# Placing the high and low parts of a three-product float32 matmul: weights at multiples of 128 bytes, their partners 64 bytes beyond

## The chip, the cores and the metric

The kernel runs on one core of a Trainium2 chip. The time is that of the device, in microseconds, from the first to the last instruction of one launch, and what is compared is the median of several runs. TensorE multiplies, ScalarE (ACT), VectorE (DVE) and GpSimd (POOL) do elementwise work, SyncE (SP) issues the DMAs. [...]

## The reference, cut to what matters

Two layers run on 1024 prompt tokens and 64 sample tokens of width 1024. Layer 0 mixes tokens with an S5 state space model, layer 1 with RWKV-7. Each is followed by cross-attention to a memory and by an MLP with a squared ReLU, with a residual and a layer norm after each:

```python
out = (z @ p["s5_w_glu_v"][j]) * jax.nn.sigmoid(z @ p["s5_w_glu_g"][j])
...
x = layer_norm(DEEPNORM_ALPHA * x + h, p["ln_g"][i, 0], p["ln_b"][i, 0])
h = memory_cross_attention(x, mem_k[i], mem_v[i], p["xa_w_q"][i], p["xa_w_o"][i])
x = layer_norm(DEEPNORM_ALPHA * x + h, p["ln_g"][i, 1], p["ln_b"][i, 1])
h = sq_relu_mlp(x, p["mlp_w1"][i], p["mlp_w2"][i])      # 1024 -> 4096 -> 1024
```

Everything is float32.

## The kernel before

The activations `x` stay in SBUF, channels on the partitions as 8 panels of 128, the 1088 tokens along the free dimension in four chunks (`CH`): three of 256 tokens and a last one of 320.

A large product isn't done in float32 outright. Each operand is split into a high part rounded to `float32r` and a low part, the rest (`split`, L70, and `wtile`, L74, for weights: ScalarE writes the high part, VectorE or GpSimd the low one). `mm3` (L65) then makes a product of three matmuls, high by high, high by low, low by high, all added up in PSUM:

```python
s.mm(ps, wh, xh, first, False)
s.mm(ps, wh, xl, False, False)
s.mm(ps, wl, xh, False, last)
```

Each of them loads 128 columns of weights (LDWEIGHTS, the row PEld of the profile) and streams 256 or 320 columns of the other operand past them (MATMUL, the row PE). The next weights are loaded while a matmul streams, so at any time TensorE reads two places in SBUF: the moving operand, and the weights of the next matmul. 20,400 of its 28,046 matmuls are such full ones.

The stages, in order: the S5 mixer (to about 318 us); its gated output `glu` (products of X, the split activations `XH`, `XL`, into the banks `pg`); layer 0's attention and MLP (`layer`, `attention`); the RWKV mixer (`rwkv_r`, `rwkv_k`, `rwkv_vg`, `rwkv_solve`, `rwkv_scan`); layer 1's attention and MLP. An MLP runs over 16 iterations of two panels of the hidden width. In each, `up` makes a chunk's hidden activations of X (48 matmuls into `pq`), `split` into `hh` and `hl`, and `down` multiplies those of one chunk before by the second weights (48 matmuls into `pg`) and adds them to the residual. An iteration holds 288 matmuls of 256 columns, half from `up` and half from `down`, and 96 of 320. Attention does the same with `qh`, `ql` (queries), `ph`, `pl` (probabilities) and `oh`, `ol` (heads' outputs); there the queries are the weights, and the memory's keys stream.

The order within an engine is made by the framework's planner, which works from the program's dependencies and its own idea of times; in the MLP it breaks `up` and `down` up into pieces of 3 to 48 matmuls and interleaves them. A tile's place is reused when the last reader of the whole tile is done (`reuse_waits="tile"`). Pools lay their tiles one after the other.

Where the parts lie follows from what was laid before them. In the compiled program of this kernel, the starts of the tiles modulo 128 bytes are:

| stage | moving part | weight part | moving less weight, modulo 128 |
|---|---|---|---|
| glu, layer 0's queries and `up` | XH, XL 96 | wh, wl 32 | 64 |
| layer 0 and 1: `down`, attention's outputs | hh, hl, oh, ol 32 | wh, wl 32 | 0 |
| layer 0 and 1: scores, values | 32 | 32 | 0 |
| rwkv_r, receptance | XH, XL 96 | wh, wl 64 | 32 |
| rwkv_r, decays and gates (64 rows) | hdh, hdl 64 | wah, wal 64 | 0 |
| rwkv_k; rwkv_vg (weights stream) | 96 | 96 | 0 |
| rwkv_scan, output product | oh, ol 96 | wh, wl 96 | 0 |
| layer 1's queries and `up` | XH, XL 32 | wh, wl 32 | 0 |

Slices of a tile (a chunk, a panel, 128 columns of weights) begin at multiples of 128 bytes from its start, so the last column holds for every matmul.

Of the kernel before, what the change touches and what calls it, by code (L numbers as in the profile page):

```python
# [9 lines left out]
F32R = mybir.dt.float32r  # L10
# [5 lines left out]
DRAM = bass.MemoryType.DRAM  # L16

ALPHA = 4.0 ** 0.25
TT = 1088
# [7 lines left out]
class Parts:  # L27
    """tiles side by side in a tile that is not in use yet"""
# [15 lines left out]
class Net:  # L44
# [29 lines left out]
    def wtile(s, src, e=None, cols=1024, rows=128):  # L74
        """A weight panel from DRAM as its two parts."""
        raw = s.raw.tile([128, 1024], F32, name="raw")[:rows, :cols]
        s.load = s.d.dma_start(out=raw, in_=src)
        hi = s.wp.tile([128, 1024], F32R, name="wh", tag="wh")[:rows, :cols]
        lo = s.wp.tile([128, 1024], F32R, name="wl", tag="wl")[:rows, :cols]
        s.a.copy(out=hi, in_=raw)  # L80
        s.lastlo = (e or s.g).tensor_tensor(out=lo, in0=raw, in1=hi.bitcast(F32), op=ALU.subtract)  # L81
        return hi, lo

    def lnexp(s):
        """both ln and exp in ScalarE's tables"""
        s.tc.keep_in_program_order(s.a.preload_act_table_set("natural_log_exp_and_others"))
# [13 lines left out]
    def banks(s, n, W, get):  # L100
        """n panels of width W as (first panel, [128, panels, W]) a bank each"""
        m = 512 // W
        for p in range(0, n, m):
            q = min(m, n - p)
            yield p, q, get(q * W).rearrange("p (j t) -> p j t", j=q)
# [37 lines left out]
    def rnd(s, out, x, scale):  # L143
        """out = the integer nearest to x * scale"""
# [5 lines left out]
    def horner(s, out, r, cs, first):  # L150
        """out = first r^n + cs[0] r^(n-1) + .. without the constant term, times r"""
# [4 lines left out]
    def expx(s, P, out, x):  # L156
        """exp to float32's accuracy"""
# [15 lines left out]
    def sincos(s, P, sn, cs, x):  # L173
        """sin and cos to float32's accuracy"""
# [12 lines left out]
        # i^k: k to -2..2, its cosine 1 - |k|, its sine k (2 - |k|)  # L187
# [14 lines left out]
    def unit(s, P, c, sn):  # L202
        """One Newton step to length 1"""
# [9 lines left out]
    def s5_setup(s, P, sm):  # L213
        """Tables of the powers of a; P holds what stays, sm the temporaries."""
# [18 lines left out]
        # powers 0..8 of a  # L233
# [15 lines left out]
        # f = (a - 1) / lambda  # L249
# [15 lines left out]
        # halves: rows 0..63 the real part, rows 64..127 the imaginary one  # L265
# [9 lines left out]
        # unit rotation by 8 steps, and its powers: lo 0..15, hi 16 * (0..7), two groups of a batch's four in the  # L275
        # rows' first half and two in the second; the sine of all of them with the sign of the first half
# [42 lines left out]
    def s5_tables(s, B, b, Tt, dr):  # L319
        """For four groups, 64 of the 1024 channels: what depends on the weights alone."""  # L320
# [29 lines left out]
        # CA[(half, s), g, tau, c]  # L350
# [11 lines left out]
        # BM[(j, c), g, (half, s)]  # L362
# [10 lines left out]
        # K[(q, c), (tau, c')] and the skip on its diagonal  # L373
# [14 lines left out]
        # rotations e^{i Theta n}, n = 16 hi + lo  # L388
# [23 lines left out]
    def s5_batch(s, B, b, U, CA, BM, T, C2, S2):  # L412
# [3 lines left out]
        # what each chunk brings to the state  # L416
# [29 lines left out]
    def s5_outputs(s, B, dr, U, CA, T, H):  # L446
        """y[(j, c), n], to memory"""
# [13 lines left out]
    def s5_gather(s, B, k, yd, X):  # L461
        """Channels to partitions (of four groups, by channel in the group, then group), the gelu, and its parts."""
# [19 lines left out]
    def s5(s, x, X, filler):  # L482
        """the tables lie in x's place"""
# [29 lines left out]
    def memkv(s, mp, kvd):  # L513
        """a panel at a time, in float32 outright"""
# [45 lines left out]
    def lnsum(s, x, p, c, acc):  # L560
        """adds panels p, p + 1 to the running sum of two columns of panels"""
# [6 lines left out]
    def lndirect(s, x, p, ps):  # L568
        """the last chunk's sum, a panel at a time, one panel late"""
# [16 lines left out]
    def lnsteps(s, x, c, li, acc, X=None, new=None, bank=None, done=None):  # L586
        """Normalise the chunk c of x in place over the channels; its parts into X."""
# [55 lines left out]
    def rsqrt(s, var, bias, eps, W, n=128, tables=True):  # L643
        """(var + eps)^-1/2: a start from the tables, or from the exponent's bits, then Newton steps"""
# [52 lines left out]
    def softmax(s, B, ps, n):  # L697
        """probabilities of the scores ps[128, n, 256]"""
# [14 lines left out]
    def attention(s, l, x, X, kvd, after, B, B1, early, begin):  # L713
        """B, B1: pools that outlive it; early, begin: what may go ahead of the end"""
        tc, v, a, g = s.tc, s.v, s.a, s.g
        s.lnexp()
        with ExitStack() as es:
# [4 lines left out]
            def query(h, c, wq):  # L722
                t0, W = CH[c]
                qh, ql = (Q.tile([128, 2, 256], F32R, name=n) for n in ("qh", "ql"))
# [17 lines left out]
            def probs(ps):  # L742
                pr = s.softmax(B, ps, 2)
                ph, pl = (B1.tile([128, 2, 256], F32R, name=n) for n in ("ph", "pl"))
# [7 lines left out]
            def values(h, c, kh, kl, ph, pl, os):  # L752
                W = CH[c][1]
                oh, ol = (B1.tile([128, 2, 320], F32R, name=n)[:, :, :W] for n in ("oh", "ol"))
# [16 lines left out]
            # the sample's queries, each sequence against its own memory: rows (sequence, 32), two banks' halves  # L771
            def load(nm, h, b):
                """two of the eight"""
# [102 lines left out]
    def layer(s, l, x, X, kvd, norm1, norm2):  # L876
        """attention and MLP, the MLP's first products ahead of the attention's last"""
        tc, v, a, g = s.tc, s.v, s.a, s.g
        NB = 16
        with tc.tile_pool(reuse_waits="tile", name="ab", bufs=2) as B, tc.tile_pool(reuse_waits="tile", name="ab1", bufs=1) as B1, ExitStack() as es:  # L880
# [5 lines left out]
            def up(i, c, w):  # L886
                t0, W = CH[c]
                hh, hl = (M[0].tile([128, 2, 320], F32R, name=n)[:, :, :W] for n in ("hh", "hl"))
# [71 lines left out]
    def shifted(s, P, c, x):  # L960
        """x at t - 1 less x at t, for chunk c, panels 4 h and on"""
# [21 lines left out]
    def mixed(s, i, c, x, d):  # L983
        """chunk c of the i-th token-shift mix, (first k, [128, k's, W]) at a time; d[h]: panels 4 h and on"""
# [7 lines left out]
    def mixes(s, c, x, d, lg, D):  # L992
        """the mixes of the keys and values, and the gates' hidden layer (in float32 outright), to memory"""
# [13 lines left out]
    def remixed(s, i, c, D):  # L1007
        """the same from memory"""
# [5 lines left out]
    def mix(s, m, c, X):  # L1014
        """its parts into X"""
# [4 lines left out]
    def chunked(s, t, q, W):  # L1020
        """[128, q, chunks, 64] of a tile that holds (chunk, q, 64)"""
        return t[:, :q * W].rearrange("p (c e t) -> p e c t", e=q, t=64)
# [4 lines left out]
    def spill(s, D, c, p, q, src, n=64):  # L1027
        """a tile of (chunk, q, n) to the panels from p on of D[chunk, 128, 8, n], and back"""
# [4 lines left out]
    def solve(s, v, M, Th, tm, n, load, store):  # L1033
        """(1 - A)^-1 of 32-blocks, a block in each of n partitions, all transposed"""
# [13 lines left out]
    def rwkv_r(s, x, X, D):  # L1048
        """decays and gates, and the receptance"""
        tc, v, a, g = s.tc, s.v, s.a, s.g  # L1050
        E = math.exp(-0.5)
        with ExitStack() as es:
# [3 lines left out]
            # of the hidden layers: the weights for x, and times the mixes for what the shift adds  # L1056
# [7 lines left out]
            wah, wal = (P.tile([128, 1024], F32R, name=n) for n in ("wah", "wal"))  # L1064
# [3 lines left out]
            hid = [P.tile([128, TT], F32R, name=n) for n in ("hdh", "hdl")]  # L1068

            def lora(c, d):  # L1070
                """the hidden layers, in float32 outright"""
# [59 lines left out]
    def rwkv_k(s, x, X, D):  # L1131
        """keys, the removal's two factors, and how a chunk's removals meet"""
        tc, v, a, g = s.tc, s.v, s.a, s.g
        E = math.exp(-0.5)
        with tc.tile_pool(reuse_waits="tile", name="k1d", bufs=1) as Q, tc.tile_pool(reuse_waits="tile", name="k1u", bufs=2) as T:
# [4 lines left out]
            # a panel's two heads apart  # L1140
# [15 lines left out]
            def unit(p, q, c, ps, cs, al):  # L1156
# [19 lines left out]
                # minus the inverse of the squared length  # L1176
# [5 lines left out]
                # the decays up to the step before  # L1182
# [18 lines left out]
            def removals(p, q, c, pmt, pm, y, kb):  # L1201
                t0, W = CH[c]
                # A_ab of the chunks, [(the chunk's parity, s), head, chunk, t]
# [51 lines left out]
    def rwkv_solve(s, P, D):  # L1255
        """in the place P"""
# [9 lines left out]
        def solve2(p0, e, *place):  # L1266
            """partitions (block, panel, head, chunk)"""
# [13 lines left out]
        def sample():  # L1281
            """partitions (block, panel, head)"""
# [15 lines left out]
    def rwkv_vg(s, x, X, D):  # L1298
        """values and output gates, time on the partitions"""
        tc, v, a, g = s.tc, s.v, s.a, s.g  # L1300
        TL = [(t, min(128, TT - t)) for t in range(0, TT, 128)]
        with tc.tile_pool(reuse_waits="tile", name="v1", bufs=1, side="right") as P:
            hid = [P.tile([128, TT], F32R, name=n) for n in ("hdh", "hdl")]
# [26 lines left out]
    def scan_setup(s, P):  # L1330
        """what the scan holds from its start on"""
        v, g = s.v, s.g
        L, U_, R2 = slice(0, 64), slice(64, 128), slice(32, 64)
        # rows 0..63 a chunk's inverse, rows 64..127 what its removals bring to the outputs
# [3 lines left out]
        # a panel's two heads apart: [(h, j), h, (a, r), panel, t]  # L1338
# [7 lines left out]
        # the bonus' factors, a panel's two heads apart  # L1346
# [6 lines left out]
        # decays over a chunk: of the prompt for rows (64 + j), of the sample for rows (b2, j)  # L1353
# [9 lines left out]
    def rwkv_scan(s, x, D):  # L1363
        """The chunks in order, all the heads at once; head hh = 8 (its half of the panel) + panel."""
        tc, v, a, g = s.tc, s.v, s.a, s.g
        L, U_, R1, R2 = slice(0, 64), slice(64, 128), slice(0, 32), slice(32, 64)
        with tc.tile_pool(reuse_waits="tile", name="r2f", bufs=1) as F, tc.tile_pool(reuse_waits="tile", name="r2", bufs=2) as B, \
# [11 lines left out]
            def heads(hf, get):  # L1379
                """eight heads' places in a bank: (head, its panel, its rows, [128, 64])"""  # L1380
# [4 lines left out]
            def prep(ci, bn=None, own=None):  # L1385
                """own: the sample's tiles"""
# [29 lines left out]
                # what of the chunk meets itself  # L1416
# [9 lines left out]
                # the bonus' weight of each head  # L1426
# [10 lines left out]
                # decayed to the chunk's end, time to partitions  # L1437
# [13 lines left out]
                # the inverse's block off the diagonal  # L1451
# [15 lines left out]
            def chain(ci, E, nxt):  # L1467
                """nxt: where the state goes, and is already without the chunk's own"""
# [21 lines left out]
            def outputs(ci, E, Y):  # L1490
                """into rows of Y: two banks"""
# [13 lines left out]
            def finish(k, Y, bn, y=None):  # L1505
                """group norm, bonus, gate, and channels to partitions"""
# [28 lines left out]
            def store(k, y, n):  # L1535
                """into the parts [k, 128, (a chunk, the sample, a chunk)]"""
# [9 lines left out]
            def out(c, p0):  # L1546
                """two panels of the mixer's output for the chunk c, the sample with the first"""
# [7 lines left out]
                for i in range(2):  # L1555
# [3 lines left out]
                    for h in range(2):  # L1559
                        wh, wl = (W.tile([128, 512], F32R, name=nm, bufs=2) for nm in ("wh", "wl"))  # L1560
# [13 lines left out]
            def norm(c):  # L1574
                """of a finished chunk of the residual"""
# [12 lines left out]
            def sample(S, Q):  # L1588
                """Eight sequences of eight tokens with their own states, a part at a time: places that end with the second
                part, and that stay."""  # L1590
# [342 lines left out]
```

## Time and profile before

| | |
|---|---|
| median of 3 runs | 3892.05 us |
| lowest and highest | 3887.28, 3900.02 us |
| span of the profiled execution | 3890.0 us |
[...]
| PE (matmul) busy | 3556.8 us, 91% |
| PEld (weight load) busy | 3334.9 us, 86% |
| DVE, ACT, POOL busy | 51%, 31%, 36% |

The page has no time of its own for the profiled execution beside its span of 3890.0 us. How to read it: successive matmuls overlap in the trace, because each is shown from its first column to the modelled end of its last. So neither the share of 91% nor the mean of one (280 to 310 ns) is what a matmul costs. In a stream without waits that is the distance from one start to the next, read from the starts of a timeline or from a piece of the chain that has its time and its number of matmuls.

### The profile page before, as it was taken

What the parts mean: (1) busy time and instruction counts of PE and PEld (TensorE: products, weight loads), DVE (VectorE), ACT (ScalarE), POOL (GpSimd) and SP (SyncE); (2) the same over time, 40 slices, a digit from 0 to 9 for tenths busy, and PEclk for the clock granted to TensorE, in tenths of its full rate; (3) what the DMA queues carried; (4) which work ended last, traced back from release to release, by engine and by line L of the source; (5) the groups of instructions that cost most, each with busy time, mean ns of one, the idle gap of its engine ahead of it and who ended that gap; (6) DMA issues with size and microseconds to landing.
All of it is one profiled execution on the core that took longest, in us unless ns stands there. A gap on an engine that the chain in (4) does not pass through costs nothing. (4 is left out here: it accounts for less than half of the span.)

```text
span 3890.0 us, 67671 instructions
## 1 busy us (share of the span) xinstructions
PE 3556.8 (91%) x28046; PEld 3334.9 (86%) x28046; DVE 1980.5 (51%) x3344; ACT 1204.7 (31%) x2299; POOL 1418.1 (36%) x1035
## 2 busy tenths in 40 slices
PE   6669979989999999979987988997899899999997
PEld 4558979979999999968875767997799799999997
DVE  9991174354333333485588656678534633333335
ACT  3662152243112111243572212234422411111113
POOL 5652251143222222433567343344312332222222
PEclk8789999999999999989998877999999999999999
DMA  4444122311111111035576635552222111111111
GB/s 137 127 135 158 33 67 82 112 67 56 44 44 44 44 44 44 30 132 158 171 209 152 192 85 163 144 155 90 88 98 87 66 44 44 44 44 44 44 39 47
DMA packets 270243, 351.22 MB, mean 90 GB/s; under 512 B 109200, under 2 KB 200848, under 8 KB 269168
## 3 DMA queue, kind: packets, MB, share of 16 engines
q1 hardware_dynamic: 269936, 346.89, 29.0%
q8 instruction: 221, 3.62, 0.4%
q14 instruction: 86, 0.70, 0.1%
HBM read 271.80 MB, written 75.01 MB: 89 GB/s over the span
## 5 line engine op out<-in xcount | busy, mean ns | idle before, releaser
L63 PE MATMUL pq<-XH,wh 128*128 128x256 f32 (+1 forms) x2944 | 856.9, 291 | 33.0 <-ACT XH L71 17.0
L57 DVE TENSOR_TENSOR x<-x,pg 128x512 f32<-128x512 f32 (+1 forms) x720 | 435.8, 607 | 840.3 <-PE pg L63 833.8
L63 PE MATMUL pq<-XL,wh 128*128 128x256 f32 (+1 forms) x2944 | 853.4, 290 | 1.6 <-DVE XL L72 1.6
L63 PE MATMUL pq<-XH,wl 128*128 128x256 f32 (+1 forms) x2944 | 851.6, 289 | 1.2 <-POOL wl L81 1.2
L81 POOL TENSOR_TENSOR wl<-raw,wh 128x1024 fp32r<-128x1024 f32 x194 | 467.2, 2418 | 1005.6 <-ACT wh L80 923.9
L63 PEld LDWEIGHTS pq<-XH,wh 128*128 128x128 f32 x2944 | 561.2, 191 | 45.9 <-ACT XH L71 19.8
L63 PE MATMUL pg<-hh,wh 128*128 128x256 f32 (+1 forms) x2048 | 593.8, 290 | 4.9 <-DVE x L57 4.9
L63 PE MATMUL pg<-hl,wh 128*128 128x256 f32 (+1 forms) x2048 | 592.0, 289 | 0.4 <-DVE hl L60 0.4
L63 PE MATMUL pg<-hh,wl 128*128 128x256 f32 (+1 forms) x2048 | 591.5, 289 | 0.0
L63 PEld LDWEIGHTS pq<-XL,wh 128*128 128x128 f32 x2944 | 561.2, 191 | 5.8 <-DVE XL L72 2.5
L63 PEld LDWEIGHTS pq<-XH,wl 128*128 128x128 f32 x2944 | 560.8, 191 | 3.2 <-POOL wl L81 1.8
L80 ACT CAST wh<-raw 128x1024 fp32r<-128x1024 f32 x209 | 215.2, 1047 | 657.3 <-PE pq L63 297.9
L63 PEld LDWEIGHTS pg<-hh,wh 128*128 128x128 f32 x2048 | 385.9, 189 | 6.2 <-DVE x L57 5.3
L63 PEld LDWEIGHTS pg<-hl,wh 128*128 128x128 f32 x2048 | 386.4, 189 | 1.7 <-DVE hl L60 0.8
L63 PEld LDWEIGHTS pg<-hh,wl 128*128 128x128 f32 x2048 | 386.0, 188 | 0.2
L54 POOL TENSOR_TENSOR tm<-tm 128x512 f32<-128x512 f32 (+1 forms) x160 | 146.8, 917 | 532.9 <-ACT tm L893 532.7
L893 ACT ACTIVATE tm<-pq 128x512 f32<-128x512 f32 (+1 forms) x160 | 84.8, 530 | 652.1 <-PE pq L63 632.0
L60 DVE TENSOR_TENSOR hl<-tm,hh 128x512 fp32r<-128x512 f32 (+1 forms) x160 | 101.5, 634 | 197.5 <-POOL tm L54 188.8
L63 PE MATMUL pg<-XH,wh 128*128 128x256 f32 (+1 forms) x640 | 187.2, 293 | 4.8 <-ACT tm L680 2.6
L63 PE MATMUL pg<-XL,wh 128*128 128x256 f32 (+1 forms) x640 | 187.0, 292 | 0.0
L63 PE MATMUL pg<-XH,wl 128*128 128x256 f32 (+1 forms) x640 | 186.5, 291 | 0.5 <-DVE wl L81 0.5
L63 PE MATMUL pg<-ol,wh 128*128 128x256 f32 (+1 forms) x512 | 147.5, 293 | 5.4 <-DVE ol L72 5.4
(474 smaller groups left out, 7049.8 us busy)
## 6 DMA issues: line engine op xcount, KB each, us to landing
raw<-in_w_dram SPq DMA_DIRECT2D x128, 512.0 KB, 3.5
raw<-in_ck_dram SPq DMA_DIRECT2D x32, 512.0 KB, 3.5
raw<-in_cv_dram SPq DMA_DIRECT2D x32, 512.0 KB, 3.5
raw<-in_w_o_dram SPq DMA_DIRECT2D x32, 512.0 KB, 3.6
raw<-in_wk_dram SPq DMA_DIRECT2D x16, 512.0 KB, 4.1
raw<-in_wv_dram SPq DMA_DIRECT2D x16, 512.0 KB, 4.2
raw<-in_wq_dram SPq DMA_DIRECT2D x16, 512.0 KB, 3.5
raw<-in_wo_dram SPq DMA_DIRECT2D x16, 512.0 KB, 5.6
```

The costliest lines, as they stand in the source:

```text
L54: e.tensor_tensor(out=out, in0=a, in1=b, op=ALU.mult)
L57: e.tensor_tensor(out=out, in0=a, in1=b, op=ALU.add)
L60: e.tensor_tensor(out=out, in0=a, in1=b, op=ALU.subtract)
L63: s.lastmm = s.t.matmul(out=out, lhsT=lhsT, rhs=rhs, start=start, stop=stop, **k)
L80: s.a.copy(out=hi, in_=raw)
L81: s.lastlo = (e or s.g).tensor_tensor(out=lo, in0=raw, in1=hi.bitcast(F32), op=ALU.subtract)
L893: a.activation(out=r, in_=ps, func=AF.Relu)
```

## The change

Two helpers place the parts. `even` makes a weight part's tile start at a multiple of 128 bytes. `odd` makes one tile that holds both parts of the other operand, starts it at a multiple of 128 and leaves out the first 16 float32 (64 bytes); the high part comes first, the low part behind it. Every length is a multiple of 128 bytes, so the low part, too, lies 64 bytes beyond a multiple of 128. The queries in the scores, which are the weights of their matmul, are made with `odd`, and the keys and values that they meet with `even`, as panels from `wtile`.

```diff
-        hi = s.wp.tile([128, 1024], F32R, name="wh", tag="wh")[:rows, :cols]
-        lo = s.wp.tile([128, 1024], F32R, name="wl", tag="wl")[:rows, :cols]
+        hi, lo = (s.even(s.wp, 1024, n)[:rows, :cols] for n in ("wh", "wl"))
...
+    def even(s, pool, n, name, **k):
+        return pool.tile([128, n], F32R, name=name, tag=name, align_bytes=128, **k)
+
+    def odd(s, pool, shape, name):
+        n = math.prod(shape[1:])
+        t = pool.tile([128, 2 * n + 16], F32R, name=name, align_bytes=128)[:, 16:]
+        names = "abcd"[:len(shape) - 1]
+        r = f"p ({' '.join(names)}) -> p {' '.join(names)}"
+        return [t[:, i * n:i * n + n].rearrange(r, **dict(zip(names, shape[1:]))) for i in range(2)]
...
-                qh, ql = (Q.tile([128, 2, 256], F32R, name=n) for n in ("qh", "ql"))
+                qh, ql = s.odd(Q, [128, 2, 256], "qhl")
...
-                ph, pl = (B1.tile([128, 2, 256], F32R, name=n) for n in ("ph", "pl"))
+                ph, pl = s.odd(B1, [128, 2, 256], "phl")
...
-                oh, ol = (B1.tile([128, 2, 320], F32R, name=n)[:, :, :W] for n in ("oh", "ol"))
+                oh, ol = (t[:, :, :W] for t in s.odd(B1, [128, 2, 320], "ohl"))
...
-                hh, hl = (M[0].tile([128, 2, 320], F32R, name=n)[:, :, :W] for n in ("hh", "hl"))
+                hh, hl = (t[:, :, :W] for t in s.odd(M[0], [128, 2, 320], "hhl"))
...
-            wah, wal = (P.tile([128, 1024], F32R, name=n) for n in ("wah", "wal"))
+            wah, wal = (s.even(P, 1024, n) for n in ("wah", "wal"))
...
-            hid = [P.tile([128, TT], F32R, name=n) for n in ("hdh", "hdl")]
+            hid = s.odd(P, [128, TT], "hid")
...
-                        wh, wl = (W.tile([128, 512], F32R, name=nm, bufs=2) for nm in ("wh", "wl"))
+                        wh, wl = (s.even(W, 512, nm, bufs=2) for nm in ("wh", "wl"))
...
-                    Xo = [W.tile([128, 8, 576], F32R, name=nm) for nm in ("oh", "ol")]
+                    Xo = s.odd(W, [128, 8, 576], "ohl")
...
-            return [xp.tile([128, 8, TT], F32R, name=nm) for nm in ("XH", "XL")]
+            return n.odd(xp, [128, 8, TT], "X")
```

`hid` is changed in the same way in `rwkv_r` and in `rwkv_vg`. The rest of the diff takes out comments. No instruction is added or taken away in the program's text.

## Rows read from the trace of the kernel before

**Rows 1.** The page's first part: busy us, share of the span, instructions of each engine.

```profile
PE 3556.8 (91%) x28046; PEld 3334.9 (86%) x28046; DVE 1980.5 (51%) x3344; ACT 1204.7 (31%) x2299; POOL 1418.1 (36%) x1035
```

**Rows 2.** Busy time by stretch: length, PE, PEld, DVE, ACT, POOL, PEclk, DMA, GB/s.

```profile
541.00:870.00 329.00, 300.52 (x2323) 276.90 (x2323) 163.72 (x273) 113.91 (x241) 95.58 (x48) 0.95 0.26 88
870.00:1640.00 770.00, 768.73 (x6135) 764.17 (x6133) 259.18 (x424) 167.01 (x258) 233.46 (x151) 1.00 0.14 45
1680.00:2745.00 1065.00, 945.78 (x8296) 825.99 (x8297) 730.48 (x1195) 370.67 (x723) 501.94 (x434) 0.91 0.52 149
2745.00:3070.00 325.00, 297.14 (x2298) 274.69 (x2297) 158.34 (x268) 113.41 (x239) 82.95 (x42) 0.95 0.25 86
3070.00:3880.00 810.00, 798.59 (x6226) 789.99 (x6224) 281.52 (x457) 184.48 (x293) 239.76 (x157) 1.00 0.13 43
```

**Rows 3.** Waits of PE in 870 to 1640 us, the longest: us, times, longest.

```profile
PE pz L765 <- ACT pT L810: 0.8, 1, 0.8
```

**Rows 4.** Chain in layer 1's MLP: start us, us, matmuls.

```profile
3219.58 5.39 PE pq L63 x45
...
3237.75 4.27 PE pg L63 x36
...
3255.31 6.59 PE pq L63 x45
...
3303.70 6.59 PE pq L63 x45
```

**Rows 5.** Timeline of PE, layer 0's MLP, the same matmul of two successive iterations.

```profile
1160.60 0.28 PE L63 MATMUL pq<-XH,wh 128*128 128x256 f32 x1
...
1208.29 0.28 PE L63 MATMUL pq<-XH,wh 128*128 128x256 f32 x1
```

**Rows 6.** Timeline of PE, layer 0's MLP, first and last of 36 matmuls.

```profile
1187.17 0.28 PE L63 MATMUL pq<-XH,wh 128*128 128x256 f32 x1
...
1191.14 0.28 PE L63 MATMUL pq<-XH,wl 128*128 128x256 f32 x1
```

**Rows 7.** Layer 0's and layer 1's MLP by operation and shape: count, busy us, mean ns.

```profile
L63 PE MATMUL pq<-XH,wh 128*128 128x256 f32 x746 | 207.0, 277 | 0.0
...
L63 PE MATMUL pq<-XH,wh 128*128 128x256 f32 x742 | 209.6, 283 | 0.0
```

**Rows 8.** Timeline of PE in rwkv_r, first and last of 8 matmuls.

```profile
1802.50 0.28 PE L63 MATMUL pq<-XL,wh 128*128 128x256 f32 x1
...
1803.32 0.28 PE L63 MATMUL pq<-XH,wl 128*128 128x256 f32 x1
```

**Rows 9.** Timeline of PE in rwkv_k, first and last of 10 matmuls.

```profile
1925.09 0.28 PE L63 MATMUL pq<-XH,wl 128*128 128x256 f32 x1
...
1926.17 0.28 PE L63 MATMUL pq<-XH,wl 128*128 128x256 f32 x1
```

**Rows 10.** Timeline of PE in rwkv_r, both tiles at 64 modulo 128, 64 rows.

```profile
1814.18 0.28 PE L63 MATMUL pg<-hdh,wah 64*128 64x256 f32 x1
...
1814.42 0.28 PE L63 MATMUL pg<-hdh,wal 64*128 64x256 f32 x1
```

**Rows 11.** Timeline of PE in glu: nine of 320 columns, then 49 of 256.

```profile
368.63 0.31 PE L63 MATMUL pg<-XH,wh 128*128 128x320 f32 x1
...
369.95 0.28 PE L63 MATMUL pg<-XH,wh 128*128 128x256 f32 x1
...
381.26 0.28 PE L63 MATMUL pg<-XH,wh 128*128 128x256 f32 x1
...
386.91 0.28 PE L63 MATMUL pg<-XH,wh 128*128 128x256 f32 x1
```

**Rows 12.** Timeline of PE in glu, after a longer gap; last two span 43 matmuls.

```profile
489.24 0.47 PE L63 MATMUL pg<-XH,wh 128*128 128x256 f32 x1
489.55 0.28 PE L63 MATMUL pg<-XL,wh 128*128 128x256 f32 x1
...
494.31 0.28 PE L63 MATMUL pg<-XL,wh 128*128 128x256 f32 x1
```

More of the change, by code (lines that the diff above doesn't have):

```diff
@@ L1302, in rwkv_vg @@
         with tc.tile_pool(reuse_waits="tile", name="v1", bufs=1, side="right") as P:
-            hid = [P.tile([128, TT], F32R, name=n) for n in ("hdh", "hdl")]
+            hid = s.odd(P, [128, TT], "hid")
             def out(nm, hf, t, n, ps):
```

## The prediction

> **What bounds the kernel.** First the shares of the engines: PE is busy 91% of the span, and no other engine above 51% [rows 1]. A share is no limit by itself, so the stretches come next. In layer 0's MLP PE is busy 768.7 of 770 us, in layer 1's 798.6 of 810; in the two attentions 91%, in the RWKV stages 89% [rows 2]. The waits agree: the longest that PE has in the first MLP is 0.8 us [rows 3]. So for 1580 us the pace of successive matmuls alone sets the time, and in the attentions nearly so. The chain of layer 1's MLP is nothing but matmuls, and it gives their pace: 45 of `up` with 256 columns in 5.39 us, 119.8 ns each; 36 of `down` in 4.27 us, 118.6 ns; 45 of 320 columns in 6.59 us, 146.4 ns [rows 4].
>
> The page can't show that this pace depends on anything; two layers that run the same code can. An iteration of layer 1's MLP takes 3303.70 - 3255.31 = 48.39 us [rows 4], one of layer 0's 1208.29 - 1160.60 = 47.69 us [rows 5]. `up` in layer 0 settles at 3.97 us for 35 steps, 113.4 ns [rows 6], and its matmuls are shown as 277 ns long, in layer 1 as 283 [rows 7]. By the table of places the parts differ in one thing: in layer 0 XH and XL lie 64 bytes from the weights modulo 128, in layer 1 they lie together. At 32 bytes (receptance) the pace is 0.82 us in 7 steps, 117 ns [rows 8]; at 0, with both at 96, 1.08 us in 9 steps, 120 ns [rows 9]; at 0 with both at a multiple of 64 still 0.24 us in 2 steps, 120 ns [rows 10]. So an even start buys nothing; the distance between the places seems to.
>
> **The change, part by part.** It adds and removes no instruction. It sets the distance to 64 everywhere.
>
> Price of one matmul. The 144 matmuls of `up` with 256 columns make the whole difference of an iteration: 0.70 us / 144 = 4.9 ns. This holds what 113.4 ns doesn't, the first matmuls of each piece, which start out slower. I take layer 0's mean, 119.8 - 4.9 = 114.9 ns, for every matmul of 256 columns that now lies at distance 0 or 32. Saved are 4.9 ns on layer 1's X and 118.6 - 114.9 = 3.7 ns on `down`, whose pace I also take for the attention's own products, which have no steady stretch.
>
> - `up` of layer 1: 16 iterations x 144 = 2304 matmuls x 4.9 ns = 11.3 us.
> - `down` of both layers: 4608 x 3.7 ns = 17.0 us.
> - Attention, both layers: layer 1's queries 8 panels x 8 x 3 parts x 3 chunks = 576 x 4.9 = 2.8 us; output products 1152 x 3.7 = 4.3 us; scores and values 32 units x 24 = 768 x 3.7 = 2.8 us. That is 9.9 us, of which I count the busy share of 91% [rows 2]: 9.0 us.
> - RWKV: keys and output product 1152 x (120 - 114.9) = 5.9 us, receptance 576 x (117 - 114.9) = 1.2 us. DVE, which PE often waits for here, is busy 730 of 1065 us [rows 2], so I count half: 3.5 us.
> - Layer 0's `up`, its queries and glu lie at distance 64 already: 0.
> - Matmuls of 320 columns: 146.4 ns at distance 0 [rows 4] and 1.32 us in nine steps, 146.7 ns, at distance 64 in glu [rows 11]: 0.
> - The streamed weights of 512 columns in rwkv_vg (486 matmuls): no row at distance 64; the nearest, 320 columns, says 0. [...]
>
> Sum 40.8 us. Against the profiled span of 3890.0 us, 2 us below the median, it gives 3849; against the median 3851 us.
>
> Costs on the other side. One tile for two parts comes free only when the last reader of both is done. In `mm3` the low part's last reader stands one matmul before the high part's, so the wait grows by at most one matmul, 0.12 us, and in the MLP the place was last read a unit of some 11 us earlier, by two buffers: nothing. The odd tiles grow by 64 bytes and move what lies behind them; for float32 tiles no distance was set before or after. The planner may order the pieces otherwise: I allow 10 us either way, a dozen waits as long as the first MLP's longest [rows 3].
>
> [...]
>
> **The rivals.**
>
> *The slow lock.* In glu all is at distance 64, as all will be, and yet its pace is not 113.4 ns: after a chunk of 320 columns, 48 steps take 5.65 us, 117.7 ns [rows 11]. Only after a gap of 0.31 us between two starts does it run at 4.76 us in 42 steps, 113.3 ns [rows 12]. So the fast pace could need a stumble before it, which layer 0's `up` gets from the slower pieces of `down` between, and which the changed MLP, without waits and with 320 columns twice in an iteration, would lack. Against it: glu shows this at one pair of places, and the new pair is another. At 117.7 ns `down` gains 0.9 x 4608 = 4.1 us, layer 1's X 2.1 x 2880 = 6.0 us, and layer 0's X loses 2.8 x 2880 = 8.1 us; attention with its waits keeps half of 9, RWKV 2. In all 8.5 us: 3883.
>
> *Slower: the places (64, 0) behave as distance 0 does.* No row has a moving part at 64 with weights at 0. If it is not the distance that counts but the pair (96, 32), all runs at 119.8 ns, and what was good is lost: layer 0's X 2880 x 4.9 = 14.1 us, glu 1152 x 2.1 = 2.4, receptance 576 x 2.8 = 1.6, `down` 4608 x 1.2 = 5.5, attention's others 1920 x 1.2 = 2.3. In all 26 us: 3918. It decides as soon as the mean pace is above about 118.5 ns.
>
> *More than layer 0 has.* 320 columns lose 6.7 ns too, as 256 columns did from 120 to 113.3. Some 4850 matmuls x 6.7 = 32 us: 3819. Against it: at distances 0 and 64 they show no difference [rows 4, 11]. [...]
>
> *The change does nothing:* the layers differ by something else than the places: 3892.
>
> *The planner or the shared tile costs:* an order with new waits, from 12 us up.
>
> **How the numbers follow.** Forecast 0.48, slow lock 0.24, slower by the places 0.10, more than layer 0 has 0.08, order or tile 0.06, nothing 0.04. What can be told from no change is about 0.3%, 12 us. Faster are the forecast, the better case and a quarter of the lock (0.06): 0.62. Same are the rest of the lock and nothing: 0.22. Slower: 0.16. The forecast's own range: if all settles at 113.3, `down` gains 24, X of both layers 2880 x 6.5 + 2880 x 1.6 = 23, glu 5, the others 14, in all 66 us: 3826; halfway to the lock 3867. The range to 3905 holds the lock and nothing, and half of the costs of order; at 3815 it holds part of the better case. Outside are most of the slower case and the rest of the better one.
>
> **What would show it.** Right: the chain of layer 1's MLP has `up` x45 in about 5.15 us and `down` x36 in 4.1; an iteration takes 47.1 us in both layers; 320 columns stay at 146. The lock: both layers at 117.7 ns and 48.0 us, layer 0 slower than before. Wrong altogether: 119.8 ns in both, or PE waiting in the MLP for a part that it didn't wait for.

## The result, and the profile after

The changed kernel takes 3857.7 us (median of 4 runs, 3844.7 to 3864.3) against 3889.7 us before (3886.3 to 3900.0): a ratio of 0.991, 95% interval 0.989 to 0.994, or -34 us (-44 to -25). The forecast was 3851 us.

The page's first part, to be held against [rows 1]: the same 28,046 matmuls, 32 us less of busy PE, the other engines changed by at most 6.5 us.

```profile
PE 3525.2 (91%) x28046; PEld 3300.9 (86%) x28046; DVE 1987.0 (51%) x3344; ACT 1204.7 (31%) x2299; POOL 1419.8 (37%) x1035
```

Busy time by stretch (length, PE, PEld, DVE, ACT, POOL, PEclk, DMA, GB/s), the two MLPs, as in [rows 2]. PE still fills them at a granted TensorE clock (PEclk) of 0.99 to 1.00, so the pace still sets the time, and the clock doesn't explain a change of pace.

```profile
865.00:1625.00 760.00, 758.59 (x6066) 754.20 (x6066) 253.21 (x418) 163.21 (x250) 230.85 (x149) 1.00 0.14 44
...
3050.00:3850.00 800.00, 787.85 (x6273) 777.75 (x6272) 285.07 (x459) 187.09 (x296) 243.28 (x158) 0.99 0.14 45
```

The longest wait of PE in layer 0's stretch is as short as in [rows 3]:

```profile
PE pz L776 <- ACT pT L821: 0.8, 1, 0.8
```

The chain in layer 1's MLP (start us, us, matmuls), to be read against [rows 4]:

```profile
3155.66 5.11 PE pq L63 x45
...
3173.20 4.28 PE pg L63 x36
...
3184.36 4.08 PE pg L63 x36
3188.87 1.39 PE pg L63 x12
3190.26 6.55 PE pq L63 x45
3196.81 4.28 PE pg L63 x36
...
3202.87 5.11 PE pq L63 x45
```

`up` (pq, 256 columns) now takes 5.11 us in place of 5.39, 113.5 ns each; 320 columns 6.55 in place of 6.59. But `down` (pg) has two speeds: 4.28 us (118.9 ns) for two chunks of 256 columns, 4.08 us (113.3 ns) for the one between. An iteration takes 3202.87 - 3155.66 = 47.21 us, before 48.39.

Layer 0 hardly gained. The same matmul of two successive iterations, and then first and last of two stretches of 36 steps of `up` in one of them (timeline of PE):

```profile
1188.24 0.45 PE L63 MATMUL pq<-X,wh 128*128 128x320 f32 x2
...
1235.84 0.45 PE L63 MATMUL pq<-X,wh 128*128 128x320 f32 x2
```

```profile
1177.83 0.28 PE L63 MATMUL pq<-X,wl 128*128 128x256 f32 x1
...
1181.90 0.28 PE L63 MATMUL pq<-X,wl 128*128 128x256 f32 x1
...
1201.43 0.28 PE L63 MATMUL pq<-X,wl 128*128 128x256 f32 x1
...
1205.67 0.28 PE L63 MATMUL pq<-X,wl 128*128 128x256 f32 x1
```

The iteration takes 47.60 us where it took 47.69 [rows 5]. `up` runs at 4.07 us / 36 = 113 ns in one chunk and at 4.24 / 36 = 117.8 ns in another, and that second pace is new in layer 0's MLP [rows 6]. It is the pace of the prediction's slow lock, and two of an iteration's three chunks of 256 columns have it: of the 46 long pieces of `up` in this MLP, 30 stand near 117.7 ns, where 45 stood near 114 before.

By stages, from the first to the last matmul of `down`: layer 0's MLP 765.1 us before, 763.5 after; layer 1's 774.3 and 757.9. From the attention's first scores to the first `down`: 328.2 and 322.6, and 318.2 and 311.8 in layer 1. From the gated output's first matmul to the first scores, with the first two of layer 0's eight panels of queries: 241.0 and 237.5. From layer 0's last `down` to layer 1's first scores, RWKV and again two panels of queries: 1115.2 and 1117.6, which is within what it varies by: 1102.8 to 1125.1 us over the kernels below, and a0_x_only and a2_hh64, which move nothing in it, have 1125.1 and 1105.0.

### The profile page after: what moved, and what is told of

Same layout as the page of the kernel before. It is cut to its first block, busy times and chain, and to the rows that moved or that the text cites. A ratio compares the mean times of both kernels' runs of the same rounds, so it can differ in the third digit from the quotient of the medians.

```text
span 3859.5 us, 67659 instructions
## 1 busy us (share of the span) xinstructions
PE 3525.2 (91%) x28046; PEld 3300.9 (86%) x28046; DVE 1987.0 (51%) x3344; ACT 1204.7 (31%) x2299; POOL 1419.8 (37%) x1035
## 5 line engine op out<-in xcount | busy, mean ns | idle before, releaser
L63 PE MATMUL pq<-X,wh 128*128 128x256 f32 (+1 forms) x5888 | 1131.2, 288 | 35.0 <-ACT X L71 17.5
L63 PEld LDWEIGHTS pq<-X,wh 128*128 128x128 f32 x5888 | 928.0, 189 | 51.5 <-ACT X L71 20.1
L63 PE MATMUL pq<-X,wl 128*128 128x256 f32 (+1 forms) x2944 | 845.5, 287 | 1.2 <-POOL wl L80 1.2
L63 PE MATMUL pg<-hhl,wh 128*128 128x256 f32 (+1 forms) x4096 | 782.3, 288 | 5.7 <-DVE x L57 5.1
L63 PEld LDWEIGHTS pg<-hhl,wh 128*128 128x128 f32 x4096 | 640.0, 188 | 8.3 <-DVE x L57 5.5
L63 PE MATMUL pg<-hhl,wl 128*128 128x256 f32 (+1 forms) x2048 | 586.5, 286 | 0.0
L63 PEld LDWEIGHTS pq<-X,wl 128*128 128x128 f32 x2944 | 557.3, 189 | 3.2 <-POOL wl L80 1.8
L63 PEld LDWEIGHTS pg<-hhl,wl 128*128 128x128 f32 x2048 | 385.8, 188 | 0.2
L63 PE MATMUL pg<-X,wh 128*128 128x256 f32 (+1 forms) x1280 | 242.0, 289 | 5.0 <-ACT tm L691 2.6
L63 PE MATMUL pg<-ohl,wh 128*128 128x256 f32 (+1 forms) x1024 | 202.3, 292 | 6.2 <-DVE ohl L72 5.0
```

Of the source, the lines that this page charges most:

```text
L63: s.lastmm = s.t.matmul(out=out, lhsT=lhsT, rhs=rhs, start=start, stop=stop, **k)
```

## Two speeds in `down`: modulo 256

The two buffers of the hidden parts give the lead. The odd tile of `down` is 5120 + 64 bytes, its buffers 5248 bytes apart, which is 20.5 times 256: alike modulo 128, not modulo 256. The places in the compiled program, in bytes modulo 256, with the paces that the trace shows (beyond wh, wl: the moving part's place less that of the weights):

| changed kernel | moving | wh, wl | beyond wh, wl | ns |
|---|---|---|---|---|
| glu, layer 0 X | 64 | 128, 128 | 192, 192 | 113.3 and 117.7 |
| layer 0 hidden, buffers 1 and 2 | 192; 64 | 128, 128 | 64, 64; 192, 192 | 117.8; 113.3 |
| layer 1 X | 192 | 0, 128 | 192, 64 | 113.5 |
| layer 1 hidden, buffers 1 and 2 | 64; 192 | 0, 128 | 64, 192; 192, 64 | 118.9; 113.3 |

The kernel before, counted in this way, had layer 0's X 192 beyond both weights, as it still is, `down` 128 beyond both, and layer 1's X 0 beyond. The prediction, counting modulo 128, called the last two distance 0 and read 118.6 and 119.8 ns there [rows 4].

Theory A: only the distance modulo 128 counts, and 113.3 or 117.7 is taken by chance. Theory B: modulo 256 counts. Rival C: the pace hangs on what ran before, not on addresses.

## The experiments

Nine kernels of the real work and two with a stretch of bare matmuls. In the diffs `odd` has three more arguments, the bytes ahead (`pad`, in floats), behind (`tail`) and the alignment; a tail on `pT`, the tile that lies just ahead of the hidden parts, sets their start. What stands behind # in a diff is a note for the reader. The runs are from three chips, so the ratios, each to the kernel before on the same chip, compare better than the times.

| kernel | ratio (95%) | mean ns, 256 columns | MLP 0, MLP 1 us |
|---|---|---|---|
| before | 1 | 118.1 | 765.1, 774.3 |
| changed | 0.991 (0.989 to 0.994) | 115.8 | 763.5, 757.9 |
| e1_same | 1.004 (1.002 to 1.006) | 119.3 | 778.0, 773.9 |
| a0_x_only | 0.997 (0.995 to 0.998) | 116.5 | 764.7, 766.0 |
| a1_hh192 | 0.994 (0.992 to 0.996) | 115.7 | 769.1, 749.9 |
| a2_hh64 | 0.995 (0.993 to 0.997) | 116.0 | 759.5, 763.5 |
| b1_l0 | 0.983 (0.980 to 0.986) | 114.1 | 749.9, 749.8 |
| b2_l1 | 0.995 (0.993 to 0.998) | 117.1 | 769.0, 767.7 |
| c1_best | 0.987 (0.985 to 0.989) | 114.0 | 749.9, 749.8 |
| c2_split | 0.986 (0.984 to 0.989) | 114.2 | 749.9, 749.9 |
| d1_mid | 0.990 (0.987 to 0.993) | 115.9 | 768.8, 749.8 |

The mean is over 15,168 matmuls, the waits (starts more than 160 ns apart) left out. One ns of it is worth 15 us, and the times follow it roughly: the change's -2.24 ns says -34 us, as measured; b1_l0's -3.9 ns says -60, measured -66 (-76 to -56). For the others the two differ by up to 13 us (a1_hh192: -36 by the mean, -23 measured), so the paces say more than the times where two kernels are close.

**e1_same: the 64 bytes taken out.**

```diff
-        t = pool.tile([128, 2 * n + 16], F32R, name=name, align_bytes=128)[:, 16:]
+        t = pool.tile([128, 2 * n], F32R, name=name, align_bytes=128)
```

> The layout of the change with the 64 bytes taken out: high and low part still in one tile, weights still at multiples of 128 bytes, and the parts they are multiplied with at multiples of 128 too (distance 0). If the distance between moving data and weights is what the change is worth (theory A: only the distance modulo 128 counts; theory B: the distance modulo 256 counts, and at 0 both say the same), every full matmul of 256 columns falls back to 119 to 120 ns, about 4 ns more than the 115.5 ns of the changed kernel on 13,800 of them: 3905 to 3920 us, slower than the kernel before, which had some of its matmuls at other distances. If the gain comes from the merged tiles or from the weights' alignment alone (rival), the time stays at 3850 to 3865 us.

Measured: 3902.4 us, ratio 1.004, slower than before, if a little less than expected; 119.8 ns in layer 0's `up`, 119.0 in layer 1's. The chain of its layer 1's MLP:

```profile
3171.14 5.36 PE pq L63 x45
3176.50 4.29 PE pg L63 x36
```

So neither the shared tile nor the even start brings anything that shows (the mean pace alone makes 19 us more, 15 were measured). The gain is that of the distance, and without it the change is a loss: layer 0's `up`, which stood at distance 64 before, loses its 114.6 ns.

**a0_x_only: the hidden parts back at distance 0.**

```diff
-                hh, hl = (t[:, :, :W] for t in s.odd(M[0], [128, 2, 320], "hhl"))
+                hh, hl = (t[:, :, :W] for t in s.odd(M[0], [128, 2, 320], "hhl", 0, 0, 64))
...
+                pT = B1.tile([128, 512 + (16, 0)[l]], F32, name="pT")[:, :512].rearrange("p (a b c) -> p a b c", a=2, b=2)
```

> The changed kernel, but the MLP's hidden parts (hh, hl) lie at a multiple of 128 again, both buffers alike (distance 0); all else keeps its 64 bytes. Theories A and B: the 4608 matmuls of 256 columns in `down` go from 116.4 and 117.2 ns to about 119.7, +14 us, so about 3871 us; `up` of layer 1 stays at 113.5 to 114. Rival C (which of two paces is taken hangs on what ran just before, not on the addresses): `up` changes its pace too, to 117.7 ns in both layers, +20 us more, about 3890 us.

Measured: 3869.8 us, `down` at 119.3 and 118.9 ns, as A and B say. `up` of layer 1 rose to 115.4 ns: its first matmuls behind each piece of `down` start slow and then fall to 113.3, so a slow neighbour costs its own part here, some 4 us (2304 matmuls, 113.5 ns in the changed kernel). Layer 0's `up` went the other way, to 114.6 ns. C's 117.7 in both layers is out, but neighbours do count.

**a1_hh192 and a2_hh64: both buffers alike modulo 256.**

```diff
-                hh, hl = (t[:, :, :W] for t in s.odd(M[0], [128, 2, 320], "hhl"))
+                hh, hl = (t[:, :, :W] for t in s.odd(M[0], [128, 2, 320], "hhl", 0, 0, 64))
...
+                pT = B1.tile([128, 512 + (0, 48)[l]], F32, name="pT")[:, :512].rearrange("p (a b c) -> p a b c", a=2, b=2)
```

(a2_hh64 has `(32, 16)[l]` there.)

> The changed kernel with the stride of the hidden parts' two buffers made a multiple of 256 bytes (5120 in place of 5248), so that both lie alike: 192 bytes beyond wh modulo 256 in both layers (hh at 64 in layer 0, at 192 in layer 1). Theory A (only modulo 128 counts; both distances are 64 modulo 128): no change, 3853 to 3863 us. Theory B (modulo 256 counts; 192 is the good distance, 64 the bad): `down` goes from 116.4 and 117.2 to 113.3 to 113.7 ns, -15 us on 4608 matmuls, and `up` of layer 0, which runs between slow buffers, from 116.1 towards 113.5, up to -6 us: 3833 to 3843 us, the quickest so far. Rival C (chance and history): paces mixed as before, 3850 to 3865 us.

> The mirror of the run before: both buffers of the hidden parts 64 bytes beyond wh modulo 256 (hh at 192 in layer 0, at 64 in layer 1). Theory A: no change, 3853 to 3863 us. Theory B: `down` at 117.7 ns in layer 0 and 119 to 120.6 in layer 1 (117.7 at the matmuls with wh, 124 at those with wl), +3 and +6 us, and `up` of layer 0 drawn to 117.7 by its neighbours, +4 us: 3867 to 3875 us, with `up` of layer 1 still at 113.5 to 114. Rival C: 3850 to 3865 us.

Measured: 3859.5 and 3861.5 us, by the times alone no more than theory A. The traces say more. Groups of a1_hh192's matmuls by operation, layer 0's MLP above, layer 1's below (count, busy us, mean ns of one; at 276 the starts stand 113 ns apart, at 281 117.7, at 283 119 to 120):

```profile
L63 PE MATMUL pg<-hhl,wh 128*128 128x256 f32 x1485 | 268.8, 282 | 0.3 <-DVE hhl L60 0.3
L63 PE MATMUL pq<-X,wh 128*128 128x256 f32 x1476 | 266.8, 281 | 0.0
...
L63 PE MATMUL pq<-X,wh 128*128 128x256 f32 x1499 | 262.3, 276 | 0.0
L63 PE MATMUL pg<-hhl,wh 128*128 128x256 f32 x1472 | 258.2, 278 | 0.3 <-DVE hhl L60 0.3
```

In layer 1, B is right: `down` from 117.2 to 113.9 ns, `up` at 113.6, the MLP 757.9 to 749.9 us. In layer 0 B is wrong: with 192 beyond wh for both operands everything sits at 117.2 to 117.6, and the MLP lost 5.6 us. In a2_hh64 layer 1's `down` went to 118.7 as B says, and layer 0 became quicker, not slower (114.4 and 116.9). What differs between the layers is wl: 128 beyond wh in layer 1, level with it in layer 0. That made theory B2: 192 beyond wh and 64 beyond wl holds 113.3, 192 beyond both keeps whichever pace it is in.

**b1_l0: wl moved by 128 bytes in layer 0; b2_l1: wl level with wh in layer 1.**

```diff
+ tc.tile_pool(reuse_waits="tile", name="gp1", bufs=1) as gp,   # ahead of the pool wp1
+                    nc.gpsimd.memset(gp.tile([128, 24], F32, name="gap"), 0.0)
```

(In b2_l1 the tile stands ahead of the pool wp3 and has 40 floats; the tails on `pT` keep the hidden parts where they were, modulo 256.)

> a1_hh192 with one more edit: a tile of 96 bytes ahead of the weight panels of the gated output and of layer 0 moves wl by 128 bytes against wh, so that X and the hidden parts lie 192 bytes beyond wh and 64 beyond wl modulo 256, as in layer 1 of a1_hh192 (there `up` ran at 113.6 and `down` at 113.9 ns; in layer 0 of a1_hh192, 192 bytes beyond both, 117.2 and 117.6). Theory B2 (it is this pair of distances that keeps the quick pace; 192 beyond both keeps whichever pace it is in): layer 0 and the gated output come to 113.5 to 114 ns; 2828 x 3.5 + 2277 x 3.7 + 1128 x 2 + 532 x 3 = 22 us below a1_hh192's 3859.5: 3832 to 3843 us. Rival (layer 0 and layer 1 differ for another reason, such as what else reads the memory at the time, and wl's place does nothing): 117 ns as before, 3855 to 3865 us.

> The mirror in layer 1: a1_hh192 with wh and wl of layer 1 both at multiples of 256 bytes, so that X and the hidden parts, at 192 modulo 256, lie 192 bytes beyond both, as in layer 0 of a1_hh192. Theory B2: `up` and `down` of layer 1 lose their steady 113.6 and 113.9 ns and run at a mix of 113.3 and 117.7, mean 115.5 to 117.6: +9 to +20 us, 3868 to 3880 us. Rival (wl's place does nothing): layer 1 stays at 113.6 to 113.9 ns and the time at 3855 to 3865 us.

Measured: b1_l0 3822.1 us, ratio 0.983, quicker than both kernels and 10 us below the expected range; b2_l1 3867.7 us. The 10 us need not be the placement's: in the profiles b1_l0's stretch of RWKV, where nothing was moved, took 1109.5 us, a1_hh192's 1119.8. The same matmul of two successive iterations of layer 0 in b1_l0, 46.67 us apart, the changed kernel's 47.60 (above):

```profile
1178.67 0.45 PE L63 MATMUL pq<-X,wh 128*128 128x320 f32 x2
...
1225.34 0.45 PE L63 MATMUL pq<-X,wh 128*128 128x320 f32 x2
```

and layer 1's chain in b2_l1, where a1_hh192 had 5.10 and 4.08:

```profile
3176.32 5.30 PE pq L63 x45
3181.62 4.24 PE pg L63 x36
```

One edit of 96 bytes took layer 0's MLP from 769.1 to 749.9 us, its mirror image took layer 1's from 749.9 to 767.7. Both MLPs of b1_l0 are equal to 0.1 us.

**p1_places: the pace by itself.** An added function runs sums of 24 matmuls on constant data ahead of the kernel:

```diff
+        for p in PLACES + PLACES[::-1]:
+            for r in range(3):
+                for _ in range(6):
+                    unit(*p, 256)
+                if r < 2:
+                    unit(*p, 320)
```

> The disputed pace by itself: the changed kernel with a stretch of matmuls on constant data put ahead of everything (its output is thrown away; the time is longer by that stretch, some 1.3 ms, and not compared). Twelve placements of (moving parts, wh, wl) in bytes modulo 512, each three times six sums of 24 matmuls of 256 columns, with one of 320 columns between, and all of it again in reverse order: (0,0,0) (64,0,0) (128,0,0) (192,0,0) (0,0,128) (64,0,128) (128,0,128) (192,0,128) (64,128,0) (192,128,0) (32,0,0) (96,0,128). Theory A (only the distance modulo 128): 119 to 120 ns wherever the moving part is 0 or 128 beyond, 113.3 or 117.7 by chance wherever it is 64 or 192 beyond. Theory B2: (192,0,128) and (64,128,0), which is the same moved by 128, at 113.3 in all six stretches; (64,0,128) and (192,128,0) at 117.7 or more; (64,0,0) and (192,0,0) at either pace. Rival C (the pace depends on what ran before or beside it, not on addresses): the same placement differs from stretch to stretch, and the first pass from the second, as much as the placements differ from each other.

Measured: the timeline of PE, for five placements (moving parts, wh, wl) the start of one matmul and of the one 120 later, in this order: (0,0,0), (192,0,0), (64,0,128), (192,0,128), (64,128,0).

```profile
32.55 0.28 PE L63 MATMUL pg<-pxh,pwh 128*128 128x256 f32 x1
...
46.95 0.28 PE L63 MATMUL pg<-pxh,pwh 128*128 128x256 f32 x1
...
186.82 0.28 PE L63 MATMUL pg<-pxh,pwh 128*128 128x256 f32 x1
...
200.95 0.28 PE L63 MATMUL pg<-pxh,pwh 128*128 128x256 f32 x1
...
303.16 0.28 PE L63 MATMUL pg<-pxh,pwh 128*128 128x256 f32 x1
...
317.43 0.28 PE L63 MATMUL pg<-pxh,pwh 128*128 128x256 f32 x1
...
438.62 0.28 PE L63 MATMUL pg<-pxh,pwh 128*128 128x256 f32 x1
...
452.22 0.28 PE L63 MATMUL pg<-pxh,pwh 128*128 128x256 f32 x1
...
494.58 0.28 PE L63 MATMUL pg<-pxh,pwh 128*128 128x256 f32 x1
...
508.19 0.28 PE L63 MATMUL pg<-pxh,pwh 128*128 128x256 f32 x1
```

14.40, 14.13, 14.27, 13.60 and 13.61 us: 120.0, 117.8, 118.9, 113.3 and 113.4 ns. B2's two quick placements hold 113.3 in all six stretches, forward and in reverse. (192,0,0) had 117.8 five times and 113.3 once, (64,0,128) 118.9 four times and 113.3 twice: these have two paces and keep one for a whole stretch. (32,0,0) had 116.7 in the first pass and 117.8 in reverse, (96,0,128) 117.8 four times and 121.1 twice. (0,0,0) was at 120.0, (64,0,0) at 117.8, (192,128,0) at 118.9, (0,0,128) at 119.1, (128,0,0) at 118.7 and (128,0,128) at 118.3 each time. So theory A is out (64 and 192 beyond aren't alike, and 0 and 128 differ a little), and C has a part: where a placement has two paces, something ahead of the stretch chooses. It isn't mere chance: (192,0,0) and (64,0,128) stand in p2_places, too, and each of their twelve stretches takes the same pace in both runs. The one quick stretch of (192,0,0), the fourth, in p1_places and in p2_places, 120 matmuls in 13.60 us each:

```profile
1165.69 0.28 PE L63 MATMUL pg<-pxh,pwh 128*128 128x256 f32 x1
...
1179.29 0.28 PE L63 MATMUL pg<-pxh,pwh 128*128 128x256 f32 x1
...
2560.35 0.28 PE L63 MATMUL pg<-pxh,pwh 128*128 128x256 f32 x1
...
2573.95 0.28 PE L63 MATMUL pg<-pxh,pwh 128*128 128x256 f32 x1
```

No other engine runs beside, and next to no DMA (1 GB/s), at a granted clock of 1.00, the upper of the two levels that the trace of the changed kernel shows (0.50 at 43 to 44 us; columns as above):

```profile
448.70:464.70 16.00, 16.00 (x137) 16.00 (x136) 0.00 (x0) 0.00 (x0) 0.00 (x0) 1.00 0.01 1
```

**p2_places and d1_mid: what about the pair?** Either each moving part counts against the weights that are loaded beside it (W; in the stretch above PEld is busy 16.00 us beside 16.00 of PE), or wl must stand 128 off wh (V). d1_mid tries W on the real kernel:

```diff
-                X = xparts(xp)
+                X = n.odd(xp, [128, 8, TT], "X", tail=32, mid=32)   # mid: floats between high and low part
```

> The same stretch as in p1_places with 24 placements of (high moving part, low moving part, wh, wl) modulo 512, forward and in reverse: all 16 with both moving parts at m = 0, 64, 128, 192, wh at 0 and wl at 0, 64, 128, 192; and eight with the low moving part 128 bytes off the high one, wl at 0 or 128. The time is not compared. Theory W (while a matmul runs, the weights of the next are loaded; what counts is how far each moving part lies from the weights loaded beside it: the high part from wh, twice of three, the low part from wl): the quick placement of before, (192, 192, 0, 128), is 192 and 64 by this count, and (192, 64, 0, 0) is too, so it must run at 113.3 in all its stretches, as quick as (192, 192, 0, 128); (64, 192, 0, 0) must run as (64, 64, 0, 128) did, 118.9 or 113.3; (64, 192, 0, 128) is 64 and 64 and must behave as (64, 64, 0, 0). Theory V (what counts is that wl lies 128 bytes off wh): no placement with wl at 0 holds 113.3, and (192, 64, 0, 0) stays at 117.8. Both: (0 or 128, the same, 0, any) at 118 to 120; wl at 64 or 192 was not seen, and no number is given for it.

> a1_hh192 with one edit in the gated output and layer 0: the low part of X begins 128 bytes later, the weights stay as they are (wh and wl both at 128 modulo 256, XH at 64, XL now at 192). Theory W: XH lies 192 beyond wh and XL 64 beyond wl, the quick pair, so `up` and the queries of layer 0 go from 117.2 to 113.6 or, with slow starts behind each piece of `down`, 114.5, the gated output from 115.6 to 113.5; `down` keeps 117.6 where it starts slow: -8 to -13 us on 2828 and 1128 matmuls, 3845 to 3853 us where a1_hh192 had 3859.5. Theory V: nothing moves, 117.2 and 115.6 ns, 3853 to 3865 us.

Measured, in the order (high part, low part, wh, wl): W falls. (192, 64, 0, 0) ran at 117.8 ns in all six stretches, (192, 192, 0, 128) at 113.3 in all six. Its timeline, one matmul and the one 120 later, for the second and then the first of these:

```profile
649.98 0.28 PE L63 MATMUL pg<-pxh,pwh 128*128 128x256 f32 x1
...
663.58 0.28 PE L63 MATMUL pg<-pxh,pwh 128*128 128x256 f32 x1
...
1111.63 0.28 PE L63 MATMUL pg<-pxh,pwh 128*128 128x256 f32 x1
...
1125.77 0.28 PE L63 MATMUL pg<-pxh,pwh 128*128 128x256 f32 x1
```

d1_mid agrees: layer 0's `up` at 117.8 ns throughout (by operation below, shown 281 ns long, as in a1_hh192's layer 0), the gated output at 117.8, slower than a1_hh192's 115.6, which V did not say either. By its 3851.2 us alone it would pass for W, but its ratio, 0.990 (0.987 to 0.993), can't be told from a1_hh192's, and no pace is W's.

```profile
L63 PE MATMUL pq<-X,wh 128*128 128x256 f32 x1472 | 266.5, 281 | 0.0
```

Of the 24 placements only (192, 192, 0, 128) always held 113.3; the next that held one pace was (64, 64, 0, 192) at 115.6, and (192, 64, 0, 128) was the slowest, 120.9. V, as far as it goes, stands: no placement with wl level with wh held 113.3. Why this one does is open.

**c1_best and c2_split: two more places, and the tile apart.**

```diff
-                    Xo = s.odd(W, [128, 8, 576], "ohl")
+                    Xo = s.odd(W, [128, 8, 576], "ohl", 16, 32)
...
+                    nc.gpsimd.memset(gp.tile([128, 32], F32, name="gap"), 0.0)   # ahead of rwkv_r's panels
```

```diff
-            X = xparts(xp)
+            X = n.apart(xp, [128, 8, TT], "X")   # c2_split, layer 1: high and low part in a tile each
```

> b1_l0 with the same pair of distances (192 beyond wh, 64 beyond wl) in two more places that had it the other way round: 128 bytes ahead of the weight panels of the RWKV receptances, and 128 bytes behind the parts of the scan's outputs, so that wh lies at 128 and wl at 0 there. By b1_l0's trace these stretches stand 2.5 and 1.6 us above 113.3 ns, with the receptances about half of the first: -3 us at most, 3815 to 3825 us where b1_l0 had 3822, too little to be told from it by the time alone; the pace of the scan's output matmuls is the test: 117.0 ns in b1_l0, 114 to 115 here. Rival (the placement found in the MLP does nothing where the matmuls run in short bursts): 117 ns as before.

> b1_l0 with high and low part of X in layer 1 in two tiles again, at the same places modulo 256 (the low part's tile begins 192 bytes later for it; the parts of the attention's outputs shift from 192 to 64, at most 2 us on 535 matmuls). Theory: that the two parts share a tile is worth nothing by itself, since each chunk's two parts are written together and read together: `up` and the queries of layer 1 at 113.6 ns as in b1_l0, and 3815 to 3832 us. Rival (a shared tile makes the first matmul wait for the low part's writer, or saves a wait): the first matmuls of each chunk in layer 1 wait by another length, and the time moves by over 10 us.

Measured: 3832.4 and 3833.9 us, ratios 0.987 and 0.986, both above the times expected. c1_best's scan outputs went from 117.0 to 115.5 ns, short of the 114 to 115 expected, X in RWKV from 115.7 to 114.3: the placement works there too, but it moves some 2.5 us, and the time does not show it. That both stand a little above b1_l0, with the same MLPs to 0.1 us, isn't explained by the places. In the profiles it lies in RWKV (1112.9 and 1118.7 us, b1_l0 1109.5) and between glu and layer 0's first `down` (558.4 and 556.9, b1_l0 555.4); RWKV's stretch varies by more between kernels with the same places in it, so b1_l0's lead may be luck. c2_split has the MLPs of b1_l0 with X in two tiles: the shared tile is worth nothing. It was tried for layer 1's X alone; e1_same bounds the rest.

## Why the prediction was right, and where its sizes were off

- *PE's pace bounds the kernel, and the distance sets the pace*: right. e1_same is the direct test: everything of the change but the 64 bytes makes it slower than before. b1_l0 and b2_l1 show the same for one pair of places at a time. But counting the distance modulo 128 was too coarse: "64 everywhere" was 64 and 192 modulo 256. In p1_places the same instructions run at 113.3 to 121.1 ns by the addresses, some placements at two paces.
- *`up` of layer 1, 11.3 us*: 119.6 to 113.8 ns (with the queries) on 2304, 13.3 us.
- *`down`, 17.0 us*: this term was mis-sized. 118.9 to 116.5 ns in layer 0 and 118.8 to 117.2 in layer 1, 5.6 + 3.7 = 9.3 us. The step took one price for all that lies at 64 modulo 128; one of the two buffers lies at the slower 64 modulo 256, and with four chunks in turn it holds two of the three chunks of 256 columns, 1536 of a layer's 2304 matmuls.
- *Layer 0's `up`, queries and glu, 0*: 114.6 to 116.1 ns on 2880 cost some 4.4 us, glu's 117.5 to 115.5 gave 2.2. X lies 192 beyond wh and wl, as it did before the change, and there p1_places has two paces. So neither comes from a change of X's distance: in a0_x_only and a2_hh64, where only `down`'s places differ, the same `up` has 114.6 and 114.4 ns.
- *Attention, 9.0 us*: 5.6 + 6.4 = 12.0 us from the first scores to the first `down`, though the first two of layer 1's eight panels of queries lie ahead of that. What part the waits have in it is not taken apart here.
- *RWKV, 3.5 us*: its matmuls of 256 columns on X went from 118.5 to 115.6 ns, but the stage shows no gain; it varies by more than that.
- *320 columns, 0*: near enough, 146.4 to 145.5 ns in layer 1's `up`, next to unchanged in layer 0, some 3 us over all. *512 columns, 0*: 227.2 to 230.9 ns where weights stream past X, some 1.8 us lost on 486.
- *Order and shared tile*: no new wait in the MLPs (the longest in layer 0's stretch 0.8 us, above); c2_split bounds the tile at nothing.

Of the rivals, the slow lock was half right: its 117.7 ns is the second pace of layer 0. "The places (64, 0) behave as distance 0 does" was wrong for 64 modulo 128, but had the right question, since 64 and 192 differ. *More than layer 0 has* did not come: 320 columns gained 0.9 ns, not 6.7. Of the signs it named, `up` x45 (5.11 us) and layer 1's iteration (47.21 us) came true, layer 0's iteration (47.60 us for 47.1) and two in three of `down` x36 (4.28 us for 4.1) did not. The mechanism was right; that the sum of 40.8 us came near 34 is partly luck, because `down`'s shortfall and X's loss were partly paid by more than was expected from layer 1's `up`, the attentions and glu.

## What to carry to other kernels

When PE runs back to back and two stretches of the same code differ by a few per cent (here 113.4 and 119.8 ns), take the pace of successive matmuls (starts over 30 or more) and put the addresses of moving operand and weights, modulo 256 at least, beside it. Try placements in a bare loop first (one run held 24 of them), and make all buffers of a tile alike: a stride of 5248 bytes, no multiple of 256, gave the second buffer another placement here (118.9 and 113.3 ns in layer 1's `down`).

## What the runs showed that was not expected

- Paces come in steps. In p1_places and p2_places stretches had 113.3, 115.6, 116.7, 117.1, 117.8, 118.2, 118.3, 118.7, 118.9, 119.1, 120.0, 120.9 and 121.1 ns, most of them the same to 0.01 ns in one stretch after the other. None was below 113.3.
- Some placements have two paces (113.3 and 117.8 ns, or 113.3 and 118.9) and keep the one they come in with over a whole stretch of 144 matmuls. In the changed kernel's layer 0 the pace goes from quick to slow across a chunk of 320 columns (36 of `down` at 113.3 ns from 1182.4 us, at 117.8 from 1194.8), and back where `up` follows a piece of `down`, with no 320 between (12 of `down` at 117.8 ns from 1175.8 us, then `up` at 113.3 after six steps at 114.3); in glu it switches both ways across a chunk of 320 (113.3 to 117.8 ns between 353 and 369 us, 117.8 to 113.3 between 401 and 417). What chooses is open.
- 320 columns depend on it less: 144.7 to 147.0 ns over the twelve placements of p1_places, 144.3 to 148.5 over the 24 of p2_places.
